# First mixer: modulations 2 to 4 as column-group products on TensorE, with their weights loaded from before the first projection

## The chip, the core and the metric

The kernel runs on one core of one Trainium2 chip. The metric is the device time of one execution in microseconds (us): a median of three runs. Engines go by the profile's names: PE (TensorE matmul) and PEld (its weight load), DVE (VectorE), ACT (ScalarE), POOL (GpSimd), SP (SyncE, which here only issues DMAs). "L498" is line 498 of the kernel before.

## What is computed

A block on 256 tokens of width 1024 (a gated linear attention and a Hyena convolution side by side, then 16 experts), followed by a second block of two layers. The change touches one small product of the first block: the modulation of the layer from the condition vector `c`.

```python
mod_x = split(silu(c) @ w_ada + b_ada, 6)        # c: 1 x 1024, w_ada: 1024 x 6144
p = modulate(rmsnorm(x), mod_x[0], mod_x[1]) @ w_in   # same for ctx, with its own mod
x = x + mod_x[2] * merge(gla(p), hyena(p)) @ w_out
hn = modulate(rmsnorm(x), mod_x[3], mod_x[4])
x = x + mod_x[5] * experts(hn)
```

Modulations 0 and 1 are needed before the projections. Modulation 2 is needed after `w_out`, modulations 3 and 4 at the experts' router and gather, modulation 5 after the experts. Each modulation reads 1024 x 1024 values of `w_ada` (4 MB, four loads of 1 MB) and multiplies them by one vector.

## The kernel before

**Stages of the first mixer** (`mixer1`, L636), in order of the trace. Up to about 47 us: filters and modulations 0 and 1 (`mods`, L436, products on PE in four column groups of 32). From 47 us: `h_transposed(0)` and `(1)` (L715) turn the tokens and the context into `hTh`, `hTl` (high and low halves), while `hy_cols(0)` (L800) and `a_cols` (L859) project them (L1111 to L1113). From about 72 us: `hy_cols(1)` beside `to_tok(0)`, `spectrum(vtok, 0)` and `gates` (L1128). Then `to_tok(1)` and `qk_cols` beside `conv_tok` (L1137), `v_cols` beside `spectrum(x1tok, 1)` (L1140), `g_cols` and `hy_cols(2)` (L1149), `conv_ch`, `w_out`.

**A projection block** (`block`, L746) reads a weight block of 512 columns as two loads of 1 MB from a ring of three slots (`slot`, L220). Each load gives two quarters. A quarter is split by `halves` (L281): ACT writes `wh` (two buffers), then POOL or DVE in turn writes `wl` (three buffers, L276). PE multiplies `wh` with `hTh` and `hTl`, and one quarter later `wl` with `hTh`. While a block runs, the next block's two loads are issued at its second half (`nxt`, L738).

**Modulations 2 to 4** (`mods_x`, L471, called at L1106) run on DVE. Each 1 MB load `wmod` (128 x 2 x 1024) is worked off by two instructions over 128 x 1024 (`scalar_tensor_tensor`, L498; the first of a modulation is a `tensor_scalar`, L496), which add `wmod` times a column of `siluc` to `modacc`. At the end of a modulation PE adds up the partitions with a matrix of ones: 8 products into `modt` for modulations 3 and 4 (result `mcf`), or 2 products of 512 columns into `modb` for modulation 2 (result `m2`), after DVE has added the bias (L513). The steps stand at every second yield of L1128's first generator and every fourth of L1137's. Loads alternate between two rooms, `D8` and `B8`.

**What sets the order.** SP's queue runs in the order in which the program is written (`block1` and `block2` are traced inside a manual schedule for SP). Inside the first mixer, from L1106 on, the order of PE, DVE, ACT and POOL is laid down when the program is built, by a planner that ranks instructions by their place in the program and by its own model of times. On the chip each engine then runs its list strictly in order. `run` (L73) steps generators in turn, `mix(a, b, n)` (L86) steps `b` once per `n` yields of `a`.

**PSUM banks** are handed out by `ps` (L208). Without a number it takes the next one of a cycle (`banks`, L204); with `hold=True` the bank is kept out of the cycle until `free`. A fixed number that is held is replaced by the next of the cycle (`while b is None or b in self.held`). A tile that is given a bank waits until the bank's earlier tile has been read for the last time.

Of the kernel before, what the change touches and what calls it, by code (L numbers as in the profile page):

```python
# [13 lines left out]
F32 = mybir.dt.float32  # L14
# [4 lines left out]
AF = mybir.ActivationFunctionType  # L19
# [4 lines left out]
D = 1024  # L24
# [48 lines left out]
def run(*gens, ratio=1):  # L73

    gens = list(gens)
    while gens:
        for i, g in enumerate(list(gens)):
            for _ in range(1 if i == 0 and len(gens) > 1 else ratio):
                try:
                    next(g)  # L80
                except StopIteration:
                    gens.remove(g)
                    break


def mix(a, b, n):  # L86

    i = 0
    for _ in a:
        yield  # L90
        i += 1
        if i % n == 0:
            next(b, None)
# [76 lines left out]
class K:  # L170
# [265 lines left out]
    def mods(self, m, cols, room):  # L436
# [31 lines left out]
        nc.vector.tensor_copy(cols, pt[:, :16].rearrange("p (k i) -> p k i", i=2))  # L468
        yield

    def mods_x(self, mods, tags, ahead=()):  # L471

        nc, p, A = self.nc, self.m1, self.A
        accs, ahead = {}, deque(ahead)

        def load(m, kp):
            src = A["w_ada"][0, kp * 256:(kp + 1) * 256, m * D:(m + 1) * D].rearrange("(k p) c -> p k c", p=128)
            if not tags:  # L480
                w = self.w(src, [128, 2, D])
                if ahead:
                    self.fetch(*ahead.popleft())
                return w
            wt = p.tile([128, 2, D], F32, name="wmod", tag=tags[kp % len(tags)])
            nc.sync.dma_start(wt, src)
            return wt

        def add(m, kp, out, wt):
            if kp == 0:  # L490
                accs[m] = p.tile([128, D], F32, name="modacc", tag=("idft", "modacc")[m % 2])
            acc = accs[m]
            for kk in range(2):
                c = self.siluc[:, 2 * kp + kk:2 * kp + kk + 1]
                if kp == kk == 0:
                    nc.vector.tensor_scalar(acc, wt[:, kk, :], c, None, op0=ALU.mult)  # L496
                else:
                    nc.vector.scalar_tensor_tensor(acc, wt[:, kk, :], c, acc, op0=ALU.mult, op1=ALU.add)  # L498

        def end(m, out):  # L500
            acc = accs[m]
            if out.shape[1] == 8:
                pt = self.ps("modt")
                for k in range(8):
                    self.mm(pt[:, k:k + 1], acc[:, k * 128:(k + 1) * 128], self.ones[:, 0:1])
                nc.vector.tensor_add(out.rearrange("p (n j) -> p n j", n=2), pt[:, :8].rearrange("p (n j) -> p n j", n=2),
                                     self.badaT[:, 2 * m:2 * m + 2])
            else:
                for nb in range(2):
                    r = 2 * m + nb  # L510
                    pt = self.ps("modb")
                    cs = slice(nb * 512, (nb + 1) * 512)
                    nc.vector.scalar_tensor_tensor(acc[0:12, cs], self.bada, self.ident[0:12, r:r + 1], acc[0:12, cs],  # L513
                                                   op0=ALU.mult, op1=ALU.add)
                    self.mm(pt, self.ones, acc[:, cs])
                    nc.scalar.activation(out[:, nb * 512:(nb + 1) * 512], pt, AF.Copy)

        last, due = None, []
        for m, out in mods:
            for kp in range(4):  # L520
                wt = load(m, kp)
                if last:
                    add(*last)
                if kp == 2 and due:
                    end(*due.pop())
                last = m, kp, out, wt
                yield
            due.append((m, out))
        add(*last)
        yield  # L530
        yield
        end(*due.pop())
# [103 lines left out]
    def mixer1(self):  # L636
        nc, A, m1 = self.nc, self.A, self.m1
# [13 lines left out]
        with self.tc.manual_schedule(engines={mybir.EngineType.PE}):  # L651
# [48 lines left out]
            m2 = m1.tile([128, D], F32, name="m2")  # L700
# [14 lines left out]
        def h_transposed(i):  # L715

            for k in range(8):
                pt = self.ps("tp")[:, 0:256]
                for t in range(2):
                    self.tr(pt[:, t * 128:(t + 1) * 128], (xn, ctx)[i][:, t, k * 128:(k + 1) * 128])  # L720
                tm = m1.tile([128, 256], F32, name="htm", tag=("lae", "aT")[k % 2])
                s_, b_ = sc[:, k, i:i + 1], mc[:, 0, k, i:i + 1]
                nc.scalar.activation(hTh[i][:, k], pt, AF.Identity, scale=s_, bias=b_)
                nc.vector.tensor_scalar(tm, pt, s_, b_, op0=ALU.mult, op1=ALU.add)
                (nc.vector, nc.gpsimd)[k % 2].tensor_tensor(hTl[i][:, k], tm, hTh[i][:, k].bitcast(F32), ALU.subtract)
                yield
# [7 lines left out]
        def flush():  # L734
            while late:
                yield from late.pop(0)
# [4 lines left out]
        def load(c0, j):  # L741
            if (c0, j) not in loaded:
                loaded[c0, j] = self.w(self.cut(W, c0, 512, 4 * j, 4), [128, 4, 512])
            return loaded[c0, j]
# [114 lines left out]
        def a_cols():  # L859

            wt = m1.tile([128, 8, 32], F32, name="wain")
            nc.sync.dma_start(wt, self.cut(W, 1536, 32, 0, 8))
            pts = [self.ps("pa") for _ in range(2)]
            whl = self.hip.tile([128, 1024], F32R, name="whl", tag="wh", bufs=2)[:, :512]
            whl = whl.rearrange("p (k i c) -> p k i c", k=8, i=2)
            self.split(whl[:, :, 0], whl[:, :, 1], wt)
            whl = whl.rearrange("p k i c -> p k (i c)")
            for k in range(8):
                for i in range(2):
                    po = pts[i][:, 0:256]  # L870
                    if k:
                        self.mm(po[0:32], whl[:, k, 0:32], hTl[i][:, k], start=False, stop=False)
                    self.mm(po[0:64], whl[:, k], hTh[i][:, k], start=(k == 0), stop=(k == 7))
                    if k == 0:
                        self.mm(po[0:32], whl[:, k, 0:32], hTl[i][:, k], start=False, stop=False)
                if k % 2:
                    yield
            a4 = m1.tile([64, 512], F32, name="a4", tag="modacc")
            for i in range(2):
                self.copy(a4[:, i * 256:(i + 1) * 256], pts[i][0:64, 0:256])  # L880
            yield
            pt = self.ps("pa")
            self.mm(pt[0:32, :], sel32[0:64], a4)
            nonlocal aT
            aT = m1.tile([33, 512], F32, name="aT", tag="aT")
            nc.vector.memset(aT[32:33, :], 1.0)
            nc.vector.tensor_copy(aT[0:32, :], pt[0:32, :])
# [215 lines left out]
        la = m1.tile([128, 4, 512], F32, name="la", tag="E8")  # L1103
        self.mcf = self.cp.tile([128, 2, 8], F32, name="mcf")
        self.m5 = self.cp.tile([128, D], F32, name="m5", tag="gb")
        mods = self.mods_x(((2, m2), (3, self.mcf[:, 0]), (4, self.mcf[:, 1])), ("D8", "B8"))  # L1106
        self.banks(range(4, 8))

        z7, z5 = [self.room(i, [128, 2, 4, 256], name="uTe") for i in (7, 5)]
        hy0 = hy_cols(0, range(4))  # L1110
        next(hy0)  # L1111
        run(h_transposed(0))
        run(chain(hy0, a_cols(), flush()), h_transposed(1))  # L1113
        mats = self.z6[:, 0:1152].rearrange("p (m c) -> p m c", m=9)
        nc.sync.dma_start(mats, A["k_mats"][:, 0:1152].rearrange("p (m c) -> p m c", m=9))
        both = self.cp.tile([128, 2, 128], F32, name="tri")
# [31 lines left out]
        mods = self.mods_x(((5, self.m5),), (), ((4,), (5, 6)))  # L1148
# [60 lines left out]
        pt = self.ps("wrc")  # L1209
# [1337 lines left out]
```

## Time and profile before

| | |
|---|---|
| time, median of 3 runs | 1628.56 us (1624.29 to 1633.93) |
| the profiled execution | 1633.42 us, of which the span of the trace is 1631.6 us |
| mean granted clock of PE | 0.958 of full speed |
| PE, DVE, ACT, POOL busy in the span | 89%, 44%, 23%, 14% |
| first mixer | from the start to about 291 us, when the experts' first products begin |

The page of the profile gives shares for the whole span. The windows view gives busy time of each engine in a stretch (its ends, its length, then busy us and instructions per engine), with the granted clock, the DMA share and GB/s; the timeline gives single instructions with, in brackets, the idle time of the engine before them and what ended it; the view of waits adds these up by releaser. A product of 32-bit floats shows as two MATMUL records (x8 is four products), one of the projections' split halves as one.

### The profile page before, as it was taken

How to read it: one execution, taken by the hardware profiler on the slowest of the kernel's cores; microseconds unless marked ns; L12 is line 12 of the kernel's file. 1: busy time of each engine (PE TensorE's matmuls, PEld its weight loads, DVE VectorE, ACT ScalarE, POOL GpSimd, SP SyncE). 2: the span in 40 equal slices, each digit the busy share in tenths (PEclk: the TensorE clock that was granted, in tenths of full speed). 3: DMA queues.
4: the chain of work that ended last, by engine and by line, in shares of the span. 5: the costliest groups of instructions: out<-in, count | busy, mean ns of one | idle time of the engine just before them, and what ended most of it. 6: DMA issues, size and time to landing. Idle time of an engine off the chain costs nothing. (4 is left out here: it accounts for less than half of the span.)

```text
span 1631.6 us, 19900 instructions
## 1 busy us (share of the span) xinstructions
PE 1457.9 (89%) x7699; PEld 771.3 (47%) x7705; DVE 712.7 (44%) x1562; ACT 372.8 (23%) x710; POOL 225.3 (14%) x139
## 2 busy tenths in 40 slices
PE   7959898988889888889999989998899999999985
PEld 2738686322224122226777744432367777444321
DVE  7897765001010000018945553432579446543324
ACT  3542243100000000005544311110245443111101
POOL 2472432000000000004212200000132222000000
PEclk9979899999997999999999989999999999899998
DMA  9536557899999999983464568999643645679995
GB/s 370 195 126 255 213 205 308 332 426 425 426 424 425 426 427 427 426 368 123 181 235 165 227 246 317 426 426 425 249 151 140 257 166 210 261 301 425 426 426 211
DMA packets 77463, 497.50 MB, mean 305 GB/s; under 512 B 9082, under 2 KB 9719, under 8 KB 23338
## 3 DMA queue, kind: packets, MB, share of 16 engines
q1 hardware_dynamic: 76136, 492.75, 74.7%
q10 hardware_dynamic: 690, 2.10, 0.3%
q0 software_dynamic: 528, 1.23, 0.3%
q8 instruction: 65, 1.06, 0.3%
q14 instruction: 44, 0.36, 0.1%
HBM read 495.00 MB, written 1.05 MB: 304 GB/s over the span
## 5 line engine op out<-in xcount | busy, mean ns | idle before, releaser
L318 PE MATMUL pg<-w,xsT 128*32 128x512 f32 (+1 forms) x1504 | 302.0, 608 | 25.1 <-DMA w<-in_w_gate_dram 14.4
L276 POOL TENSOR_TENSOR wl<-w,wh 128x1024 fp32r<-128x1024 f32 x47 | 118.5, 2523 | 494.7 <-ACT wh L275 380.1
L318 PEld LDWEIGHTS pg<-w,xsT 128*32 128x32 f32 (+1 forms) x1504 | 78.5, 118 | 203.6 <-issue 136.5
L318 PE MATMUL py<-w,hh 128*32 128x512 f32 x512 | 128.1, 599 | 23.0 <-DMA w<-in_w_down_dram 23.0
L318 PE MATMUL pu<-w,xsT 128*32 128x512 f32 x512 | 126.0, 598 | 17.4 <-DMA w<-in_w_up_dram 17.4
L318 PE MATMUL py<-w,hidT 128*32 128x512 f32 (+1 forms) x496 | 125.9, 624 | 16.0 <-DVE hidT L2282 7.9
L275 ACT ACTIVATE wh<-w 128x1024 fp32r<-128x1024 f32 x98 | 103.3, 1060 | 131.2 <-PE pj L318 50.9
L318 PE MATMUL pj<-wh,xTp 128*128 128x512 f32 (+1 forms) x448 | 123.2, 407 | 0.6 <-ACT cn L1726 0.6
L276 DVE TENSOR_TENSOR wl<-w,wh 128x1024 fp32r<-128x1024 f32 x51 | 73.0, 1432 | 59.0 <-ACT wh L275 45.5
L1407 DVE TENSOR_TENSOR hh<-hh,pu 128x512 f32<-128x512 f32 x8 | 5.4, 687 | 213.5 <-PE pu L318 213.5
L318 PEld LDWEIGHTS pj<-wh,xTp 128*128 128x128 f32 x448 | 80.6, 198 | 19.2 <-issue 3.5
L318 PEld LDWEIGHTS py<-w,hh 128*32 128x32 f32 x512 | 29.7, 108 | 117.5 <-DMA w<-in_w_down_dram 63.4
L1406 ACT ACTIVATE hh<-pg 128x512 f32<-128x512 f32 x8 | 4.8, 597 | 338.1 <-PE pg L318 230.0
L318 PEld LDWEIGHTS py<-w,hidT 128*32 128x32 f32 (+1 forms) x496 | 32.3, 124 | 90.2 <-issue 54.6
L318 PEld LDWEIGHTS pu<-w,xsT 128*32 128x32 f32 x512 | 28.3, 109 | 97.0 <-DMA w<-in_w_up_dram 48.3
L2299 DVE SCALAR_TENSOR_TENSOR yhl<-py,gs,yhl 128x512 fp32r<-128x512 f32 x44 | 32.6, 749 | 94.5 <-ACT yhl L2298 94.5
L1431 DVE SCALAR_TENSOR_TENSOR y<-py,gs,m 128x512 f32<-128x512 f32 x8 | 6.0, 751 | 146.4 <-PE py L318 146.0
L2273 ACT ACTIVATE hid<-pg 128x256 f32<-128x256 f32 x22 | 8.5, 385 | 247.0 <-PE pg L318 247.0
L318 PE MATMUL pj<-wl,xTp 128*128 128x512 f32 (+1 forms) x224 | 60.6, 391 | 0.3 <-DVE wl L276 0.3
L2312 DVE TENSOR_TENSOR y<-y,sct 128x512 f32<-128x512 f32 x88 | 56.1, 681 | 10.6 <-PE sct L318 10.1
L318 PE MATMUL ga<-S,xh 128*128 128x384 f32 (+1 forms) x160 | 53.1, 348 | 5.5 <-DVE S L2223 5.5
L2298 ACT ACTIVATE yhl<-py,gs 128x512 fp32r<-128x512 f32 x44 | 29.8, 687 | 116.0 <-PE py L318 112.2
(628 smaller groups left out, 2381.4 us busy)
## 6 DMA issues: line engine op xcount, KB each, us to landing
w<-in_expert_w_gate_up_dram SPq DMA_DIRECT2D x126, 1024.0 KB, 13.1
w<-in_w_up_dram SPq DMA_DIRECT2D x64, 1024.0 KB, 19.5
w<-in_w_down_dram SPq DMA_DIRECT2D x64, 1024.0 KB, 19.6
w<-in_w_gate_dram SPq DMA_DIRECT2D x62, 1024.0 KB, 19.6
w<-in_expert_w_down_dram SPq DMA_DIRECT2D x62, 1024.0 KB, 14.0
w<-in_w_in_dram SPq DMA_DIRECT2D x38, 1024.0 KB, 5.0
wmod<-in_w_ada_dram SPq DMA_DIRECT2D x12, 1024.0 KB, 5.6
wmod<-in_w_ada_dram SPq DMA_DIRECT2D x13, 512.0 KB, 8.5
```

The source lines that it names most:

```text
L275: nc.scalar.activation(hi, src, AF.Copy)
L276: (eng or nc.vector).tensor_tensor(lo, src, hi.bitcast(F32), ALU.subtract)
L318: self.nc.tensor.matmul(out, lhsT, rhs, start=start, stop=stop)
L1406: nc.scalar.activation(hs, pg[nb], AF.Silu)
L1407: nc.vector.tensor_mul(hs, hs, pu[nb])
L1431: nc.vector.scalar_tensor_tensor(y[:, cs], py[nb], Gs[g][1], m5[:, cs], op0=ALU.mult, op1=ALU.mult)
L2273: nc.scalar.activation(hid, pg[:, 0:256], AF.Silu)
L2298: nc.scalar.activation(yh[:, c], py, AF.Copy, scale=gs)
L2299: nc.vector.scalar_tensor_tensor(yl[:, c], py, gs, yh[:, c].bitcast(F32), op0=ALU.mult, op1=ALU.subtract)
L2312: nc.vector.tensor_add(acc[:, t, c], acc[:, t, c], pt)
```

## The change

`mods_pe` takes the place of `mods_x` for modulations 2 to 4. For each load it issues four products (two halves of the columns, two blocks of rows) with a column of `siluc`, repeated 32 times, as the stationary operand, into the four column groups of one held PSUM bank `modps`. After four loads ACT copies the bank to `modrow`, and the selection matrix `sel` brings the groups together: 8 products into `modt` (then a `tensor_add` with the bias `badaT`), or, for modulation 2, two products of 512 columns into `modb` and two more with 12 rows that add the bias.

The first two loads are issued before `h_transposed(0)`. The next load but one is issued after the products of each load. The steps stand at every third yield of L1113's first generator, then at every second of L1128's, which is 7 and 8 steps of 15. The loads go to `D8` and `C8`, then `D8` and `B8`. The two banks of `a_cols` are now held until they are copied.

```diff
+    def mods_pe(self, mods, tags):
+        nc, p, A = self.nc, self.m1, self.A
+        todo = [(m, kp) for m, _ in mods for kp in range(4)]
+        ahead, tags = deque(), deque(tags)
+        def load(i):
+            if i < len(todo):
+                m, kp = todo[i]
+                ahead.append(p.tile([128, 2, D], F32, name="wmod", tag=tags.popleft()))
+                nc.sync.dma_start(ahead[-1], A["w_ada"][0, kp * 256:(kp + 1) * 256, m * D:(m + 1) * D]
+                                  .rearrange("(k p) c -> p k c", p=128))
+        load(0)
+        load(1)
+        yield
+        for i, (m, kp) in enumerate(todo):
+            wt = ahead.popleft()
+            if kp == 0:
+                pt = self.ps("modps", hold=True)
+            for kk in range(2):
+                c = self.siluc[:, 2 * kp + kk:2 * kp + kk + 1].to_broadcast([128, 32])
+                for nb in range(2):
+                    j = 2 * kk + nb
+                    self.mm(pt[32 * j:32 * j + 32, :], c, wt[:, kk, nb * 512:(nb + 1) * 512], start=(kp == 0), stop=(kp == 3))
+            load(i + 2)
+            yield
+            if kp < 3:
+                continue
+            row = p.tile([128, 512], F32, name="modrow", tag="idft")
+            nc.scalar.activation(row, pt, AF.Copy)
+            self.free(pt)
+            out = dict(mods)[m]
+            if out.shape[1] == 8:
+                pt = self.ps("modt")
+                for k in range(8):
+                    self.mm(pt[:, k:k + 1], row[:, (k % 4) * 128:(k % 4 + 1) * 128],
+                            self.sel[:, 2 * (k // 4):2 * (k // 4) + 1])
+                nc.vector.tensor_add(out.rearrange("p (n j) -> p n j", n=2), pt[:, :8].rearrange("p (n j) -> p n j", n=2),
+                                     self.badaT[:, 2 * m:2 * m + 2])
+            else:
+                for nb in range(2):
+                    r = 2 * m + nb
+                    pt = self.ps("modb")
+                    self.mm(pt, self.sel[:, 2 * nb:2 * nb + 1].to_broadcast([128, 128]), row, start=True, stop=False)
+                    self.mm(pt, self.ident[0:12, r:r + 1].to_broadcast([12, 128]), self.bada, start=False, stop=True)
+                    nc.scalar.activation(out[:, nb * 512:(nb + 1) * 512], pt, AF.Copy)
+            yield
...
-            pts = [self.ps("pa") for _ in range(2)]
+            pts = [self.ps("pa", hold=True) for _ in range(2)]
...
+                self.free(pts[i])
...
-        mods = self.mods_x(((2, m2), (3, self.mcf[:, 0]), (4, self.mcf[:, 1])), ("D8", "B8"))
+        mods = self.mods_pe([(2, m2), (3, self.mcf[:, 0]), (4, self.mcf[:, 1])], ("D8", "C8") * 3 + ("D8", "B8") * 3)
         self.banks(range(4, 8))
...
         hy0 = hy_cols(0, range(4))
         next(hy0)
+        next(mods)
         run(h_transposed(0))
-        run(chain(hy0, a_cols(), flush()), h_transposed(1))
+        run(mix(chain(hy0, a_cols(), flush()), mods, 3), h_transposed(1))
```

## Rows read from the trace of the kernel before

**Rows 1.** Windows: PE, PEld, DVE, ACT, POOL busy, clock, DMA share, GB/s.

```profile
47.10:72.36 25.26, 22.67 (x163) 19.57 (x163) 20.83 (x34) 14.86 (x25) 14.12 (x12) 0.93 0.46 175
72.36:97.10 24.74, 21.52 (x122) 15.12 (x120) 24.64 (x25) 13.85 (x24) 12.40 (x6) 1.00 0.50 170
97.10:119.00 21.90, 7.00 (x29) 4.01 (x28) 21.90 (x17) 8.18 (x11) 20.31 (x9) 0.66 0.42 132
119.00:142.00 23.00, 22.98 (x152) 19.32 (x152) 16.54 (x16) 5.26 (x7) 4.81 (x2) 0.89 0.78 287
142.00:175.60 33.60, 33.59 (x153) 26.55 (x152) 30.34 (x30) 10.99 (x16) 16.47 (x8) 1.00 0.64 241
```

**Rows 2.** Waits of PE, 70 to 126 us: total us, times, longest.

```profile
PE tt L322 <- DVE uTe L813: 14.4, 3, 9.3
PE hyp L318 <- DVE wl L276: 2.9, 1, 2.9
```

**Rows 3.** DVE groups by line, 70 to 154 us: busy us, mean ns.

```profile
L498 DVE SCALAR_TENSOR_TENSOR modacc<-wmod,siluc,modacc 128x1024 f32<-128x1024 f32 x21 | 39.0, 1858 | 0.2
L496 DVE TENSOR_SCALAR modacc<-wmod,siluc 128x1024 f32<-128x1024 f32 x3 | 4.1, 1355 | 0.0
L513 DVE SCALAR_TENSOR_TENSOR modacc<-bada,ident,modacc 12x512 f32<-12x512 f32 x2 | 3.0, 1547 | 0.0
```

**Rows 4.** DVE timeline: start us, us, line and operation, two accumulations.

```profile
71.42 1.28 DVE L498 SCALAR_TENSOR_TENSOR modacc<-wmod,siluc,modacc 128x1024 f32<-128x1024 f32 x1
...
99.18 4.48 DVE L498 SCALAR_TENSOR_TENSOR modacc<-wmod,siluc,modacc 128x1024 f32<-128x1024 f32 x1
```

**Rows 5.** POOL timeline, first spectrum, gates and the next wl.

```profile
87.09 2.13 POOL L925 TENSOR_TENSOR ytm<-X,FB 1x512 f32<-1x512 f32 x1 [9.06 <-DVE ytm L915]
...
98.03 3.33 POOL L926 TENSOR_TENSOR X<-X,ytm 128x1024 f32<-128x1024 f32 x1
...
106.96 1.71 POOL L931 TENSOR_TENSOR Y<-X 128x512 f32<-128x512 f32 x1
108.63 5.56 POOL L975 TENSOR_TENSOR la<-la,uTe 128x1024 f32<-128x1024 f32 x2
114.15 3.34 POOL L276 TENSOR_TENSOR wl<-w,wh 128x1024 fp32r<-128x1024 f32 x1
```

**Rows 6.** PE timeline: prices of products, and the places of three chains.

```profile
21.06 1.07 PE L318 MATMUL modps<-wmod,silu 128*32 128x512 f32 x8
...
78.32 1.13 PE L318 MATMUL dft<-vtok,dft 128*128 128x512 f32 x2
...
107.59 3.46 PE L318 MATMUL modb<-modacc,tri 128*128 128x512 f32 x4 [0.51 <-DVE modacc L513]
...
119.52 1.91 PE L318 MATMUL idft<-X,dft 128*128 128x512 f32 x2
...
138.66 1.84 PE L318 MATMUL modt<-tri,modacc 128*128 128x1 f32 x16
...
181.28 3.78 PE L318 MATMUL bT<-mats,la 128*128 128x256 f32 x8 [5.31 <-DVE v L311]
...
221.64 1.95 PE L318 MATMUL modb<-modacc,tri 128*128 128x512 f32 x4 [0.94 <-DVE modacc L513]
```

**Rows 7.** Timeline of SP's DMA queue around the first projection's loads.

```profile
29.88 28.77 SPq L231 DMA_DIRECT2D w<-in_w_in_dram  x3
58.75 0.38 SPq L862 DMA_DIRECT2D wain<-in_w_in_dram  x1
```

**Rows 8.** ACT timeline: high half of the first projection's third quarter.

```profile
57.03 1.05 ACT L275 ACTIVATE wh<-w 128x1024 fp32r<-128x1024 f32 x1
```

**Rows 9.** The page, DMA issues: KB each, median us to landing.

```profile
wmod<-in_w_ada_dram SPq DMA_DIRECT2D x12, 1024.0 KB, 5.6
```

**Rows 10.** The page, 40 slices of 40.8 us: GB/s that the DMAs moved.

```profile
GB/s 370 195 126 255 213 205 308 332 426 425 426 424 425 426 427 427 426 368 123 181 235 165 227 246 317 426 426 425 249 151 140 257 166 210 261 301 425 426 426 211
```

**Rows 11.** Waits of SP's DMA queue, 0 to 300 us, L263: expert loads.

```profile
SPq L263 <- PE wo L318: 11.8, 1, 11.8
```

## The prediction, made before the change was run

> **What bounds the kernel now.** I read the view of windows first, stage by stage, because the busy shares of the whole span say nothing about one stage. In the stretch that the change is about, 72.36 to 142.0 us (69.64 us), PE is busy for 21.52 + 7.00 + 22.98 = 51.5 us and idle for 18.1 us, nearly all of it between 97.1 and 119.0, where DVE is busy for every microsecond, POOL for 20.31 of 21.9, and PE's granted clock has fallen to 0.66 [rows 1]. The reader is to see that PE is full in the stretch before it and the one after it (33.59 of 33.60 us), and that here it is DVE. The view of waits names who releases PE: 14.4 us in three waits of the transposes `tt` for `uTe`, 2.9 us for a `wl`, both written by DVE [rows 2].
>
> What fills DVE there is the work that the change removes: 39.0 + 4.1 + 3.0 = 46.1 us of the 84 us from 70 to 154 [rows 3]. It costs more than its own length because POOL works beside it: the same accumulation over 128 x 1024 takes 1.28 us early on and 4.48 us while POOL works through the spectrum's chain [rows 4, 5]. PE's order is fixed, so a `tt` that waits for DVE holds all the projections behind it.
>
> After this mixer the kernel is bound by its expert loads: in slices 9 to 17 the DMAs move some 426 GB/s without a break [rows 10], and one of the first expert loads waits 11.8 us for the mixer's last product `wo` [rows 11]. The same number of loads can run ahead of that point before and after, so I take what the mixer gains or loses to reach the end one to one.
>
> **The change, part by part.**
>
> *Removed from DVE:* all 46.1 us. That is worth nothing by itself. It is worth the idle of PE that it causes: at most 18.1 us, plus the time lost at the lower clock that follows the idle. The clock was 0.89 in 119 to 142 and 0.66 in the stretch before, so at full clock the 22.98 us would be some 2.5 us shorter and the 7.00 us, without `modb`, some 1.2 us: 3.7 us.
>
> *Removed and moved on PE:* `modb` leaves this stretch, 3.46 us at the lower clock. One `modt`, 1.84 us, comes in from the next stretch; the other, at 138.66, stays in this one [rows 6].
>
> *Added to PE:* four column-group products for each of twelve loads. The kernel already has this operation: eight records, which is one load's four products, took 1.07 us at full clock [rows 6]. Six loads come into 47 to 72 us and six into 72 to 142: 6.4 us in each. Two more products of `modb` add the bias with 12 rows; I price them like the other two (1.95 us for two at full clock [rows 6]), so modulation 2's end costs 3.9 us, now ahead of 72 us. All of this is on the path, since PE is the engine that then sets the end.
>
> The page "TensorE: Matmul & The Clock Gate" of the Trainium skill, section "Measured speedup vs the span model", speaks against the change here: it measures 3.07 times for four packed tiles and 2.38 for three. Against the 0.98 us of a full-width product in rows 6 the row of 1.07 us for four is 3.7 times. By the page's 3.07 a load would be an estimated 1.28 us and the twelve 2.5 us dearer. The row is of this kernel and the same shapes, so the sum stays with it.
>
> *Stretch 47 to 72 us.* It gains 6.4 + 3.9 = 10.3 us of PE work. PE is idle there for 25.26 − 22.67 = 2.6 us, and the clock of 0.93 costs 1.6 us [rows 1]. The first two loads are issued some 20 us before, so their 2.1 us of products can lie in the idle; half of the clock's loss may return. That leaves 10.3 − 2.1 − 0.8 = 7.4 us; the bounds are 10.3 − 2.6 − 1.6 = 6.1 and, with no cover, 10.3.
>
> *SP's queue.* Here the change adds waits. The second half of the first projection's weights is issued at 29.88 today; the row's other loads and the small `wain` follow it, and the last of the three leaves just before 58.75, when its ring slot is free [rows 7]. After the change the third modulation load stands ahead of that second half, and it waits for the products of the first load, on PE, to free `D8`. Everything queued behind it waits as well. The weights are split at 57.03 [rows 8] and a load takes 5.6 us [rows 9]; the load ahead of it adds some 2.5 us (1 MB at 426 GB/s [rows 10]), so both must leave by about 49 us to be there. The first products can run from 47 us on, in PE's gaps: I take no cost of their own, and up to 4 us if the planner puts them behind the first quarter. That end lies inside the bound of 10.3. Later loads wait two deep on PE: about 6.7 us (5.6 + 1.07) for two loads, some 34 us for the last ten. PE has 22.67 + 21.52 + 22.98 = 67 us of other work in the stretches where they lie [rows 1], so they are covered; without that cover each would be up to 3.4 us of idle.
>
> *PSUM.* The bank held for modulation 3 is one of 4 to 7 when `hy_cols(1)` asks for these by number. By my count of the cycle it is bank 5, so the projection's second column block lands in bank 0 of the other group, which the first spectrum's second `dft` needs too. That `dft`, and what follows from it, must wait until the projection's second block has been evacuated, where the first `dft` now starts at 78.32 us [rows 6]: 72.4 + 7.4 (below) + the 21.5 us of PE work that now stand before 97.1 make 101 us, the new products taking the place of what has to wait. From the first `dft` to the end of POOL's last combination (108.67) it is 30.4 us today [rows 5, 6], so `idft` could start at about 132 us; PE has projections to do until then. A part of the chain is already done by then and POOL is no longer slowed by DVE, so I take 2 us of stall, between 0 and 5.
>
> *After 142 us* the second `modt` is gone: −1.84 us, and the stretch is full of PE work, so it counts. The idle of 5.31 us before `bT`, which waits for DVE's copy of `v` [rows 6], I leave as it is.
>
> The sum: 72 to 142 us −18.1 − 3.7 − 3.5 + 1.8 + 6.4 = −17.1; PSUM stall +2.0; 47 to 72 us +7.4; after it −1.8. Together −9.5 us. Against the profiled execution, 1633.4 us, that is 1623.9. That execution lies 4.9 us above the median of the runs, and nothing in the sum depends on that, so the median becomes 1628.56 − 9.5 = 1619.1 us.
>
> **The rivals.**
>
> *Most of it is given back (about 1625 us).* The stall before `idft` is 5 us and nothing of the 10.3 us is covered, because SP holds the second half of the weights back: −17.1 + 5 + 10.3 − 1.8 = −3.6 us, 1625. For it: the fixed order of PE, which turned such a misjudgement into 14.4 us already [rows 2], and the serial queue. Against it: PE has more independent work in reach than before.
>
> *More is gained (about 1613 us).* The second spectrum's chain also loses DVE work beside it (the last eight accumulations lie after 132 us), so the copy of `v` comes earlier and the 5.31 us before `bT` close; `bT`, 3.78 us for eight records behind the idle, may be shorter by up to half at the full clock: I take 1 us. −9.5 − 6.3 = −15.8 us, 1613. Against it: other work stands ahead of the copy in DVE's fixed order.
>
> *Slower (about 1637 us).* POOL's list becomes the bound. The displaced spectrum ends at 132 us; the gates' two sums take 5.56 us and the next `wl` 3.34 us [rows 5]. If the planner keeps that order, with the `wl` behind them, the `qk` projection gets its first low half at 141 us and not at 117.5 as now. Of the 23 us that PE worked after 119 [rows 1] I take 10 to be still open then: 151 us, which is 9 us later than now; with −1.8 and about a microsecond of late spectrum it is +8.2 us, 1637. It decides from the point where that `wl` stands behind the sums in POOL's list. Against it: POOL would stand idle for long before it, and a planner fills that.
>
> **How the numbers follow.** Forecast 0.45, with its own range 1615 to 1624 (terms 6.1 to 10.3 and 0 to 5, and the spread of the three runs); given back 0.25; more gained 0.18; slower 0.12. Half a per cent, about what a measurement of this kernel can tell from no change, is 8.1 us, so faster begins below 1620.4. Two thirds of the forecast and all of "more gained" lie there: 0.30 + 0.18 = 0.48. The rest of the forecast, "given back" and a little of "slower" lie within: 0.42. Slower keeps 0.10. The range goes from 1610, the third case with the scatter of the runs, to 1632, which leaves most of the last case out.
>
> **What would show it.** Right: in the windows of the changed kernel, DVE is no longer full between 72 and 132 us, the wait of `tt` for `uTe` is gone from the waits of PE, the clock stays near 1.00, and the work that now starts at 142 us starts near 132. The twelve loads' products take about 1.07 us each. `modt` and `modb` stand before 132 us. Wrong, by step: `hyp` products of the second half waiting for `w` or PE for `wmod` (SP's queue); `idft` waiting for POOL (banks); first low half of `qk` late (POOL's list); PE full but starting `pv` later than 136 us (the price of the products); or the mixer ending earlier while the expert stage does not.

## The result: slower by 1.0%

The changed kernel takes 1649.2 us (median; 1638.9 to 1651.2) where the kernel before takes 1631.8 us on the same chip (the 1628.56 us given above is the median of the first three of these executions). The ratio is 1.0102, with a 95% interval of 1.0077 to 1.0126: about 16.6 us slower, taking 1630 us for the whole, as all differences below that come from a ratio do. The forecast was 9.5 us faster, with a range that ended at 1632.

Two profiled executions show where it went. Their spans are 1631.6 and 1646.4 us, and up to the first product of the first projection (`hyp`) they agree: it starts at 50.00 before and at 49.82 after. From there I follow five landmarks in PE's timeline, each as the start of the first such record less the start of the first `hyp`:

| us after the first `hyp` | before | after | later by | added since the last landmark |
|---|---|---|---|---|
| first `dft` of the first spectrum (`vtok`) | 28.3 | 42.9 | 14.6 | +14.6 |
| its first `idft` | 69.5 | 81.4 | 11.9 | −2.7 |
| first `dft` of the second spectrum (`x1tok`) | 92.0 | 110.5 | 18.5 | +6.6 |
| first `bT` | 131.3 | 145.2 | 13.9 | −4.6 |
| first product of the experts (`pg`) | 240.9 | 254.3 | 13.4 | −0.5 |

From `pg` to the end it is 1340.7 us before and 1342.3 after. So the loss arises in two places, ahead of the first spectrum and behind its `idft`, and the experts pass it on nearly one to one.

### The profile page after: what moved, and what is told of

It is laid out like the page before. It is cut to its first block, busy times and chain, and to the rows that moved or that the text cites. A ratio compares the mean times of both kernels' runs of the same rounds, so it can differ in the third digit from the quotient of the medians.

```text
span 1646.4 us, 20064 instructions
## 1 busy us (share of the span) xinstructions
PE 1478.1 (90%) x7799; PEld 777.8 (47%) x7805; DVE 667.6 (41%) x1536; ACT 374.7 (23%) x713; POOL 217.5 (13%) x139
## 5 line engine op out<-in xcount | busy, mean ns | idle before, releaser
L276 DVE TENSOR_TENSOR wl<-w,wh 128x1024 fp32r<-128x1024 f32 x51 | 70.2, 1376 | 69.5 <-ACT wh L275 54.4
L318 PEld LDWEIGHTS pj<-wh,xTp 128*128 128x128 f32 x448 | 80.4, 197 | 19.9 <-issue 3.6
L318 PEld LDWEIGHTS pu<-w,xsT 128*32 128x32 f32 x512 | 28.3, 109 | 95.9 <-issue 47.9
```

Of the source, the lines that this page charges most:

```text
L276: (eng or nc.vector).tensor_tensor(lo, src, hi.bitcast(F32), ALU.subtract)
L318: self.nc.tensor.matmul(out, lhsT, rhs, start=start, stop=stop)
```

## Profile after

The same stretches by the view of windows (length, then busy us of PE, PEld, DVE, ACT and POOL, granted clock, DMA share, GB/s), first of the kernel before, cut at its landmarks:

```profile
50.00:78.32 28.32, 26.47 (x199) 24.18 (x199) 24.38 (x38) 15.84 (x26) 15.77 (x13) 0.95 0.57 211
78.32:119.52 41.20, 23.05 (x103) 13.86 (x103) 41.10 (x31) 18.57 (x28) 30.32 (x13) 0.81 0.42 139
119.52:142.02 22.50, 22.49 (x152) 18.82 (x151) 16.04 (x16) 5.28 (x7) 4.81 (x2) 0.89 0.78 285
```

and of the changed kernel, with the stretch of [rows 1] in which DVE was full:

```profile
49.82:92.74 42.92, 36.27 (x223) 24.31 (x224) 22.30 (x37) 16.22 (x28) 13.34 (x12) 0.93 0.50 184
92.74:131.22 38.48, 32.21 (x204) 20.33 (x202) 16.66 (x20) 20.02 (x29) 15.93 (x9) 0.99 0.74 292
131.22:160.31 29.09, 26.18 (x143) 20.76 (x143) 5.89 (x9) 5.28 (x7) 15.33 (x8) 0.72 0.10 37
...
97.10:119.00 21.90, 19.75 (x132) 13.81 (x131) 10.34 (x15) 11.04 (x17) 4.51 (x3) 1.00 0.97 385
```

The reader is to see that what the change was for did come about: between 97.1 and 119 DVE is busy for 10.34 us and not for 21.90, PE for 19.75 and not for 7.00, at a clock of 1.00 and not 0.66. But PE has 9.8 us more to do ahead of the first spectrum (36.27 against 26.47) and is idle there for 6.65 us where it was for 1.85; and the low clock has moved to the stretch behind `idft`, 0.72 where it was 0.89.

What PE waits for now, from 70 to 165 us (total us, times, longest):

```profile
PE idft L318 <- POOL X L980: 3.9, 1, 3.9
PE dft L318 <- DVE uTe L863: 2.2, 1, 2.2
PE idft L318 <- POOL Y L981: 1.4, 1, 1.4
PE idft L318 <- POOL X L979: 1.4, 1, 1.4
```

The 14.4 us of `tt` for `uTe` [rows 2] are gone. In their place stand waits of the spectrum's own chain. PE's timeline shows both places (start us, us, operation, count; in brackets the idle time before it and what ended it):

```profile
55.89 1.04 PE L318 MATMUL modps<-wmod,siluc 128*32 128x512 f32 x2 [1.05 <-DVE htm L774]
...
58.22 1.06 PE L318 MATMUL modps<-wmod,siluc 128*32 128x512 f32 x6
...
68.36 0.38 PE L318 MATMUL hyp<-hTh,wh 128*128 128x256 f32 x1 [2.52 <-ACT wh L275]
...
79.19 1.02 PE L318 MATMUL modb<-modrow,sel 128*128 128x512 f32 x2
...
114.29 1.10 PE L318 MATMUL dft<-vtok,dft 128*128 128x512 f32 x2 [2.15 <-DVE uTe L863]
...
131.22 2.08 PE L318 MATMUL idft<-X,dft 128*128 128x512 f32 x2 [3.91 <-POOL X L980]
...
134.75 2.07 PE L318 MATMUL idft<-X,dft 128*128 128x512 f32 x2 [1.45 <-POOL X L979]
...
140.13 3.41 PE L318 MATMUL modt<-sel,modrow 128*128 128x1 f32 x16
...
194.97 3.34 PE L318 MATMUL bT<-mats,la 128*128 128x256 f32 x8 [2.55 <-DVE v L311]
```

The first load's products run only at 55.89 and 58.22, in two pieces. A `hyp` at 68.36 waits 2.52 us for its high half. The displaced `dft` stands at 114.29, waiting for the projection's evacuation, as foretold for bank 0, and the chain behind it reaches `idft` only at 131.22, when PE has been idle for 3.91 us; from there the products run at half the clock (0.50 from 131.2 to 146.6; `idft` takes 2.07 us, against 1.02 at the full one below). And SP's queue, in the same view, shows what held the weights:

```profile
30.25 29.45 SPq L483 DMA_DIRECT2D wmod<-in_w_ada_dram  x3
59.75 1.59 SPq L231 DMA_DIRECT2D w<-in_w_in_dram  x3
```

The third modulation load waits for the first one's products, and the second half of the first projection's weights, issued at 29.88 before [rows 7], leaves at 59.75.

## Experiments

All ratios are to the kernel before, on the same chip; in the diffs, "..." marks lines left out. The same landmarks for all kernels (us after the first `hyp`; two values are two profiled executions of one kernel):

| | before | after | banks | queue | both | none | modulation 2 |
|---|---|---|---|---|---|---|---|
| `dft` of `vtok` | 28.3 | 42.9 | 46.7 | 42.2 | 37.7, 39.9 | 28.0 | 27.9, 27.9 |
| first `idft` | 69.5 | 81.4 | 80.4 | 81.8 | 69.5, 74.6 | 51.3 | 57.8, 59.2 |
| `dft` of `x1tok` | 92.0 | 110.5 | 104.4 | 108.4 | 93.9, 100.3 | 78.8 | 81.5, 83.1 |
| first `bT` | 131.3 | 145.2 | 139.1 | 142.9 | 128.5, 135.0 | 113.4 | 118.1, 117.7 |
| first `pg` | 240.9 | 254.3 | 245.6 | 246.3 | 233.1, 242.9 | 215.2 | 227.9, 223.8 |

The two profiles of the kernel with both edits lie up to 9.8 us apart, and PE's granted clock differs where they part: 0.95 and 0.85 between the `dft` of `vtok` and `idft`, 0.95 and 0.92 between `bT` and `pg`. So a single profile is read here for what waits on what, and a size is taken from the ratios.

### The bank put back (e1_banks)

The projection's second column block takes bank 0 by name, where the changed kernel put it by displacement, and the cycle takes bank 5 in its place, so that the spectrum's `dft` needs no bank that a projection holds.

```diff
-        self.banks(range(4))
-        run(mix(chain(hy_cols(1, range(4, 8)), flush()), mods, 2), ...
+        self.banks((1, 2, 3, 5))
+        run(mix(chain(hy_cols(1, (4, 0, 6, 7)), flush()), mods, 2), ...
```

> The changed kernel with one thing undone: the second projection takes banks 4, 0, 6, 7 and the work beside it cycles through 1, 2, 3 and 5, so that the bank held for modulation 3 displaces nothing that the first spectrum needs. Bank theory (the displaced block holds up the first spectrum and idft, and that is most of the loss): the last dft of vtok starts before 102 us and not at 114.3, the first idft before 122 and not at 131.2, the clock does not fall to 0.50 there, and 8 to 14 of the 16.6 us come back, which leaves 3 to 9 us over the kernel before. Queue theory (the late second half of the first projection's weights is most of it): at most 3 us come back. Price theory (the products themselves cost TensorE 15 us and more, and the idle that they were to replace is not there): at most 3 us come back, and idft waits for something else.

Measured: ratio 1.0033 (1.0004 to 1.0062), 5.4 us over before: 11.2 of the 16.6 us come back (0.0069, to about ±0.004). The timeline of PE:

```profile
106.22 1.88 PE L318 MATMUL dft<-vtok,dft 128*128 128x512 f32 x4
...
131.50 0.36 PE L322 MATMUL tt<-ident,uTe 128*128 128x128 f32 x1 [3.56 <-ACT uTe L859]
135.58 1.02 PE L318 MATMUL idft<-X,dft 128*128 128x512 f32 x2
```

This execution's first `hyp` starts 5.4 us later than that of the changed kernel, so 106.22 answers to 100.8 there: the last `dft`, the second product of this row, runs some 12 us ahead of 114.29 and waits for nothing. The place that I expected for `idft` was missed: it stands at +80.4, no earlier than in the changed kernel, because it is behind the projection's work in PE's order. What it no longer does is wait for POOL, so the clock does not fall: 1.02 us and not 2.08. The gain therefore arises behind `idft`: 6.1 us by `x1tok` and by `bT`. These 6.1 us count in a first stretch that is 3.8 us longer in this execution, at a clock of 0.80 and not 0.93; from the `dft` of `vtok` to that of `x1tok` it takes 57.7 us and not 67.6. In the changed kernel the waits that name this chain add up to 2.15 + 3.91 + two of 1.45 = 9.0 us, and the half clock costs about a microsecond for each of four pairs of `idft` and 1.5 for `modt` (3.41 us, against 1.95 for the one before it), some 5.5 us together; less the 3.56 us of `tt` that are left here, that is about 11 us.

### The queue put back (e2_queue)

The second half of the first projection's weights is issued ahead of the modulations' first loads.

```diff
         next(hy0)
+        load(1568, 1)
         next(mods)
```

> The changed kernel with one thing undone: the second half of the first projection's weights is issued ahead of the modulation loads, as it was before the change. Queue theory: the high half of the third quarter is made near 59 us and not at 67.3, the first dft of vtok comes 4 to 7 us earlier, and 4 us or more come back. Bank theory: the same is gained up to the first dft, but the last dft still waits for the second projection's evacuation, so the first idft moves by less than 5 us and 0 to 5 us of the 16.6 come back. Price theory: 0 to 3 us.

Measured: ratio 1.0055 (1.003 to 1.008), 9.0 us over before: some 7.6 us come back. The 2.52 us of `hyp` for `wh` are gone from the waits of PE. The place was missed: the first `dft` of `vtok` comes 0.7 us earlier and not 4 to 7. PE's idle ahead of it does fall, from 6.65 to 3.03 us, but the stretch ran at a clock of 0.82 and not 0.93, and PE's work there took 39.22 us and not 36.27. The profile shows 2.1 us by `x1tok` and 2.3 by `bT`; the rest of what is gained by `pg` arises behind `bT`, which neither edit touches and where the clock was 0.97 and not 0.91. So the queue costs something between 2 and 8 us, and this run leaves the size open.

### Both edits, twice (e3_both, e7_both_again)

> Both of these undone. Bank and queue theory together: 12 to 20 us come back, so the time lies between 4 us over and 4 us under the kernel before, or lower if the 9.5 us that were forecast are there after all. Price theory: it stays 8 us or more over the kernel before, with TensorE busy some 20 us more than before and its idle only some 5 us less.

> The variant with both flaws undone once more, for a narrower interval and a second profile. Its first profile had the mixer's middle, from the first product of the first projection to the first dft of x1tok, 2 us longer than before the change (93.9 against 92.0 us), and the stretch after it 5 us shorter. If that holds, the two together lie 0 to 5 us under the kernel before; if the stretch after it was luck of the clock, at 0 to 4 us over.

Measured: ratios 1.0021 (0.9983 to 1.0059) and 1.0016 (0.9989 to 1.0043); their mean is 3.0 us over before. The two edits together give back 13.6 us, less than the sum of each alone (11.2 + 7.6 = 18.8), so they overlap. SP's queue is as it was meant (first of the two executions):

```profile
27.33 2.78 SPq L231 DMA_DIRECT2D w<-in_w_in_dram  x2
31.12 32.41 SPq L483 DMA_DIRECT2D wmod<-in_w_ada_dram  x3
```

and PE waits neither for the late `wh` nor for POOL any more. Of the two cases named for the second run its time fell into the second: what the first profile gained behind `x1tok` was the clock. And still the change gains nothing: with both of its faults undone it is within what can be measured of the kernel before. Two faults were real, but they were not what stood between this change and a gain.

### No early loads (e4_late)

All twelve loads and their products stand beside `hy_cols(1)`, one step at each yield, and none ahead of the first projection.

```diff
-        mods = self.mods_pe([(2, m2), (3, self.mcf[:, 0]), (4, self.mcf[:, 1])], ("D8", "C8") * 3 + ("D8", "B8") * 3)
+        mods = self.mods_pe([(2, m2), (3, self.mcf[:, 0]), (4, self.mcf[:, 1])], ("D8", "B8") * 6)
...
         next(hy0)
-        next(mods)
...
-        run(mix(chain(hy0, a_cols(), flush()), mods, 3), h_transposed(1))
+        run(chain(hy0, a_cols(), flush()), h_transposed(1))
...
-        run(mix(chain(hy_cols(1, range(4, 8)), flush()), mods, 2), ...
+        next(mods)
+        run(mix(chain(hy_cols(1, range(4, 8)), flush()), mods, 1), ...
```

> The products alone, without the early loads: all modulation loads and products stand beside the second projection, one step at each of its yields, with rooms D8 and B8 only; the first projection and its queue are as before the change, and no bank is held when the second projection asks for its own. Bank and queue theory: both delays are gone; the first stretch ends as before the change (first dft of vtok near 78 us), and the time is 0 to 12 us under the kernel before. Price theory: it is 5 us or more over it, since twelve loads in two rooms and some 13 us of products stand in TensorE's list beside the second projection.

Measured: ratio 1.0048 (1.0018 to 1.0079), 7.8 us over before. The first spectrum is early again (`dft` at +29.1, `idft` at +61.9), but PE now waits for the loads, which come one at a time into two rooms (view of waits):

```profile
PE modps L318 <- DMA wmod<-in_w_ada_dram: 4.1, 2, 2.2
```

The time lies where the price theory had it (5 us or more over) and not where the bank and queue theory did (0 to 12 under). These waits are 4.1 us of the 7.8; so with queue and banks out of the way in another manner, the loads' landing takes part of their place, and the time comes out no better than with both edits.

### None of it (e5_none)

Modulations 2 to 4 are left out altogether, loads, products and sums; their results are set to zero. It bounds what moving them off DVE, with nothing else changed, could give.

> The changed kernel without modulations 2 to 4: their loads, products and sums are left out, and the two results are set to zero. It measures what all of this costs on any engine, since everything else stays. Jam theory (before the change, VectorE's accumulations cost TensorE the 18 us of idle and the lower clock behind it): 14 to 24 us under the kernel before. Price theory (most of that idle has other causes and would be there without the accumulations): 0 to 8 us under it. What the products cost follows from its distance to the variant with both flaws undone: by the sum of rows some 17 us.

Measured: ratio 0.9895 (0.985 to 0.9939), 17.1 us under before (10 to 24 by the interval). The prediction had taken 27.1 us for the same removal (18.1 of idle, 3.7 of clock, 3.5 of `modb`, and 1.8 of `modt` in the stretch behind). The waits of PE show why it is less:

```profile
PE pqk L318 <- DVE x1tok L311: 7.0, 1, 7.0
PE tt L322 <- ACT uTe L859: 4.2, 1, 4.2
PE bT L318 <- DVE v L311: 2.5, 1, 2.5
```

With DVE free, the first spectrum's chain takes 23.3 us from `dft` to `idft` and not 41.2. But PE then stands for 4.2 us before the transposes `tt`, which wait for the projection's evacuation by ACT, and for 7.0 us before a product of `qk` that has nothing to do with `x1tok` but for its bank: the bank holds a `tt`, DVE is to copy it to `x1tok`, and DVE waits for POOL. POOL's timeline and DVE's:

```profile
113.01 4.63 POOL L1026 TENSOR_TENSOR la<-la,uTe 128x1024 f32<-128x1024 f32 x2
```

```profile
117.68 0.69 DVE L311 COPY x1tok<-tt 128x512 f32<-128x512 f32 x1 [8.05 <-POOL la L1026]
```

`x1tok` lies in the room of a summand of the gates' second sum, which ends at 117.64. Of 20.0 us of idle from the first `hyp` to `x1tok` (92.02 less 72.01 busy) 12.4 us are still there (78.80 less 66.45). By `x1tok` the profile shows 13.2 us of gain, where the prediction had 25.3, and by `bT` 17.9. The 25.7 us by `pg` are not a size of the change: between `bT` and `pg` PE is idle for 7.2 us here and 7.4 before, and the clock was 0.98 and 0.90.

The mean of the kernels with both edits is 20.1 us above this one. That is what the new work costs with its faults undone; the prediction had 15.6 us for it (7.4 + 6.4 + 1.8), within the two intervals. It is work, and not waits: up to `x1tok` PE is busy for 87.9 us in the first profile with both edits and for 66.4 here, and idle for 6.1 us and 12.4.

### Modulation 2 alone (e6_m2, e8_m2_again)

What jammed DVE first was modulation 2, whose accumulations end with `modb` at 107.59 in the kernel before [rows 6]. Here only it goes to PE, beside `hy_cols(1)`, with the bank for `modps` taken from the spectrum's group; modulations 3 and 4 stay on DVE, moved on to the next stage, beside `qk_cols`.

```diff
-        mods = self.mods_pe([(2, m2), (3, self.mcf[:, 0]), (4, self.mcf[:, 1])], ("D8", "C8") * 3 + ("D8", "B8") * 3)
+        mods2 = self.mods_pe([(2, m2)], ("D8", "B8") * 2)
+        mods = self.mods_x(((3, self.mcf[:, 0]), (4, self.mcf[:, 1])), ("D8", "B8"))
...
         next(hy0)
-        next(mods)
...
-        run(mix(chain(hy0, a_cols(), flush()), mods, 3), h_transposed(1))
+        run(chain(hy0, a_cols(), flush()), h_transposed(1))
...
-        run(mix(chain(hy_cols(1, range(4, 8)), flush()), mods, 2), ...
+        next(mods2)
+        run(mix(chain(hy_cols(1, range(4, 8)), flush()), mods2, 3), ...
...
-        run(mix(chain(qk_cols(range(6)), flush()), mods, 4), conv_tok(x1tok))
+        run(mix(chain(qk_cols(range(6)), flush()), mods, 2), conv_tok(x1tok))
```

> One part of the change alone: modulation 2 as products on TensorE beside the second projection, its four loads issued only then; modulations 3 and 4 stay accumulations on VectorE, beside the qk projection and after it. TensorE gets 4 x 1.07 + 3.9 us less the old modb, 5 to 6 us, and VectorE loses 20 of the 46 us, those that stood in the full stretch. If the jam is a matter of that stretch alone, 6 to 12 us under the kernel before; if the other 26 us, which now all lie from 119 us on, only move the jam, 0 to 6 us over it.

> The same kernel as the run with modulation 2 alone on TensorE, timed again in more rounds. If its gain of 0.4% is one of the chain and not of chance, the ratio lies between 0.993 and 0.999 again, and the first idft follows the first hyp by 55 to 62 us (69.5 before the change, 57.8 in the first run of this kernel). If the gain was chance, the ratio lies within 0.998 to 1.002 with an interval over 1.

Measured: ratios 0.9962 (0.9933 to 0.999) and 0.9958 (0.993 to 0.9986), 6 to 7 us under the kernel before, and so faster than the kernel before and the changed one. The windows of the second execution, cut at its landmarks:

```profile
54.88:82.78 27.90, 27.67 (x201) 25.66 (x202) 20.17 (x37) 17.12 (x27) 15.88 (x12) 0.91 0.43 158
82.78:114.10 31.32, 28.88 (x118) 13.65 (x118) 17.59 (x21) 18.15 (x28) 23.89 (x13) 0.84 0.54 202
114.10:138.00 23.90, 23.90 (x171) 20.87 (x169) 17.93 (x15) 5.78 (x8) 7.39 (x3) 0.92 0.71 264
```

From the first `hyp` to `x1tok` PE is idle for 2.7 us of 83.1, where it was for 20.0 of 92.0 before. DVE is busy for 17.6 us of the middle stretch and for 17.9 of 23.9 in the last one: there the accumulations of modulations 3 and 4 run without holding PE up. PE takes only the work that fills its own idle time. By `bT` the gain is 13 to 14 us, against 17.9 for leaving everything out, and the time shows half of it. The profile shows one place where some is given back: DVE, full from 165 to 188 us in the second execution, comes late to the copy of `S`, and PE waits 5.7 us for it (1.7 us before, 1.8 without the modulations).

```profile
PE upd L318 <- DVE S L1059: 5.7, 1, 5.7
```

So the jam has partly moved on. In these executions the first `hyp` also comes 8.3 and 4.9 us later than in the one before, at a clock of 0.65 and 0.77 in the 26 to 29 us ahead of it (0.98 before), which no edit touches. Where the rest goes stays open.

### The gates' sums on DVE (e9_none_sums, e10_m2_sums, e11_both_sums)

Is POOL's list what stands behind DVE? The two sums over 128 x 1024 go to DVE, in the kernel without modulations 2 to 4 (results zero), in that with modulation 2 on PE, and in that with both edits.

```diff
-                nc.gpsimd.tensor_tensor(la[:, 2 * j:2 * j + 2], la[:, 2 * j:2 * j + 2], es[j], ALU.add)
+                nc.vector.tensor_tensor(la[:, 2 * j:2 * j + 2], la[:, 2 * j:2 * j + 2], es[j], ALU.add)
```

> The kernel without modulations 2 to 4 (loads, products and sums left out, results zero), and the gates' two sums over 128 x 1024 done by DVE and not by POOL. Theory: the next limit behind the removed work is POOL's list: x1tok lies in the room of one of the summands, so its copy waits for the second sum (113.01 to 117.64 in the run without modulations, copy at 117.68), and with it the bank of tt and PE for 7.0 us. Then PE's wait of 7.0 us for x1tok falls under 2 us, the first dft of x1tok comes 72 to 76 us after the first hyp (78.8 there), and the ratio lies at 0.984 to 0.988 (0.9895 there). Rival: the spectrum's own chain is the limit and the sums only fill a gap: then PE waits 4 us or more for idft or x1tok by another name, and the landmark stays at 77 to 80 us.

> The kernel with modulation 2 alone on TensorE, and the gates' two sums on DVE and not on POOL. Theory (sums on POOL hold x1tok): x1tok's copy comes some 5 us earlier, but PE was idle for only 2.7 us there, so at most 2 us are gained: dft of x1tok at 80 to 83 us after the first hyp (81.5 and 83.1 there), ratio 0.994 to 0.998. Rival (the sums delay the whole stage): the landmark at 76 to 79 us and a ratio of 0.990 to 0.994.

> The changed kernel with the banks and SP's queue put back, and the gates' two sums on DVE and not on POOL. Theory: with both faults undone PE is nearly full there (6 us idle up to x1tok), so freeing POOL is worth 0 to 3 us: ratio 1.000 to 1.003, dft of x1tok 92 to 100 us after the first hyp. Rival (POOL's list is what keeps this change from gaining): the landmark under 91 us, ratio 0.994 to 0.999.

Measured, in this order: ratios 0.9883 (0.9855 to 0.9912), 0.995 (0.9929 to 0.9972) and 1.0015 (0.999 to 1.004); the `dft` of `x1tok` at 77.5, 83.1 and 102.1 us after the first `hyp`. None differs from its kernel with the sums on POOL by more than the intervals. In the first, the wait for `x1tok` is gone, as the theory had it, but the landmark is where the rival had it, and the waits of PE and DVE's timeline say why:

```profile
PE tt L322 <- DVE uTe L863: 9.9, 1, 9.9
```

```profile
95.20 7.42 DVE L1026 TENSOR_TENSOR la<-la,uTe 128x1024 f32<-128x1024 f32 x2 [3.25 <-ACT uTe L1025]
```

The sums, 7.42 us on DVE, hold up the evacuation of `uTe`, and `tt` waits 9.9 us where it waited 4.2. PE's idle up to the landmark is 11.9 us (77.53 less 65.67 busy), as good as the 12.4 before. That longer wait is made by the place to which the sums were moved, so this run does not show what the stage would gain if POOL's sums were out of the way altogether. What the two runs show is that some 12 us of idle stay ahead of the landmark with no accumulation on DVE, behind ACT and POOL in one order and behind DVE in the other. This is why taking all the accumulations away is worth 17 us and not 27. With modulation 2 on PE the time and the landmark are where the theory had them; with both edits the time is, and the landmark is 2 us later than its range.

## Why the prediction was wrong, step by step

The three parts of the sum beside what the runs give for them, each from ratios (to some 5 to 8 us):

| | predicted | measured |
|---|---|---|
| all that is removed | −27.1 | −17.1 (none) |
| the work that is added, without faults | +15.6 | +20.1 (both less none) |
| faults: banks, queue | +2.0 and 0 | +13.6 (after less both) |
| together | −9.5 | +16.6 |

*The PSUM term was mis-sized, by some 9 us.* The displacement was found, with its bank and its wait. That `idft` was put at about 132 us and came at 131.22 is luck: the displaced `dft` was put at 101 us and stood at 114.29, and what follows from it was taken at 30.4 us and took 16.9. It was priced at 2 us (0 to 5) because "PE has projections to do until then". It had none left ahead of `idft` in its order: it waited 9.0 us in four places, and then paid some 5.5 us of half clock, which the prediction had seen in the kernel before (0.89 behind the idle) and did not charge again to an idle of its own making. Undone, the time falls by 11.2 us. The chain itself was also longer than taken: from the first `dft` to the last combination, 30.4 us by [rows 5, 6], it is now 46.7, because one of its inputs comes at 114.29.

*SP's queue was taken at no cost of its own.* The step "the first products can run from 47 us on, in PE's gaps" failed. They were put at 55.89 and 58.22, the weights left at 59.75, which is ten microseconds behind the 49 us that the prediction itself had named as the latest, and `wh` came 2.52 us late for `hyp`. The end of "up to 4 us" held for that wait; the time says 2 to 8.

*The stretch to the first spectrum was outside its bounds*, +14.6 us for 6.1 to 10.3. Six loads' products came there, as said; but the view of groups (49.8 to 92.7 us; busy, mean ns) has 8.3 us for them and not 6.4:

```profile
L318 PE MATMUL modps<-wmod,siluc 128*32 128x512 f32 x48 | 8.3, 603 | 2.2 <-DMA wmod<-in_w_ada_dram 1.2 <-DVE htm L774 1.1
```

Two loads' products were cut into pieces, which costs more than its share (last section). `modb` took 4.2 us (3.9 predicted). And instead of covering 2.6 us, PE's idle grew by 4.8. The step that failed is "their 2.1 us of products can lie in the idle".

*The gain was taken whole, some 10 us too high.* The 18.1 us of idle were all put down to DVE; without the accumulations 7.6 of the 20.0 us up to `x1tok` went. The last wait in front of PE did end with DVE, but others stood close behind: the evacuation of the projection and the gates' sums on POOL, 11.2 us in the run without the modulations, 9.9 when the sums were moved. What is late next when DVE is not entered the sum nowhere; for this stretch only the rival "slower" asked it, of POOL's list.

*What held.* DVE is no longer full there, the wait of `tt` is gone, the clock in that stretch is 1.00. A load's products take 1.06 us (1.07 predicted). The Trainium skill, "TensorE: Matmul & The Clock Gate", section "Measured speedup vs the span model", gives 3.07 times for four packed tiles, which there are row tiles of 32; its row for column tiles has three, at 2.38. For four column groups it is 3.7 here, 1.06 us against 0.98 for one full-width product [rows 6], so the trace's price held and the page's row did not carry over. `modt` and the stretch behind it give 4.6 us: the 1.84 predicted, and half of the idle before `bT`, 5.31 to 2.55, which is the half of the rival "more is gained" that came true, in every kernel run here. The experts pass the rest on one to one.

*The rival "slower" was right in sign and half right in its place.* It put the stop at POOL's list, where the gates' sums stand ahead of what PE needs. POOL's timeline of the changed kernel:

```profile
131.14 2.33 POOL L977 TENSOR_TENSOR X<-X,ytm 128x1024 f32<-128x1024 f32 x1
133.44 1.25 POOL L979 TENSOR_TENSOR X<-Y 128x512 f32<-128x512 f32 x1
134.66 2.33 POOL L1026 TENSOR_TENSOR la<-la,uTe 128x1024 f32<-128x1024 f32 x1
136.96 1.25 POOL L981 TENSOR_TENSOR Y<-X 128x512 f32<-128x512 f32 x1
```

One sum (134.66) does stand inside the spectrum's chain and the third pair of `idft` waits 1.45 us behind it. But the first `idft` waited for the combination that ends at 131.2, late because of the bank, and the `qk` products waited behind `idft` in PE's own order, not for a `wl`. What the sums hold up when PE is not full is `x1tok`, as the run without the modulations shows.

## What to carry to other kernels

Before moving work off a full engine, ask what a kernel without that work would gain, and run it: here it gains some 17 us, and the work in its new place costs some 20. Move only the part that stands in the jam (one modulation of three), and put it where the engine that takes it is idle. And when an idle time is created on PE, charge the slow products behind it as well.

## What the runs showed of the hardware

*A piece of a column-group product costs what the whole costs.* Four products into four column groups take 1.06 us together; the one product that was cut off and ran alone at 55.89 takes 1.04 us, and the three left of that load, at 58.22, 1.06. A planner that slips another instruction between the four pays for the load twice.

*The same idle of PE is followed by either clock.* In the two executions of the kernel with both edits PE waits 2.0 us for the same instruction, and the products after it run at half the clock in one (the first row) and at the full one in the other:

```profile
28.94 2.08 PE L318 MATMUL dft<-eo,dft 128*128 128x512 f32 x2 [2.00 <-DVE FA L681]
```

```profile
28.79 1.12 PE L318 MATMUL dft<-eo,dft 128*128 128x512 f32 x2 [1.99 <-DVE FA L681]
```

The first `hyp` starts at 54.55 in the first and at 49.89 in the second, 4.66 us apart: from these rows to it PE is busy for 22.14 us at a clock of 0.77 in one and for 17.35 at 0.98 in the other. It is why places were compared from the first `hyp` on, and sizes by ratios. The later stretches vary as well, and not the same way: the second execution has the lower clock in them, and from the first `hyp` to `pg` it takes 9.8 us longer.

*POOL is faster when DVE is quiet.* `X<-X,ytm` over 128 x 1024 takes 2.33 us in the changed kernel (the row at 131.14 above) and took 3.33 beside the accumulations [rows 5]. The Trainium skill, "SBUF — State Buffer", section "Who interferes with whom", says that a DVE instruction with two SBUF inputs contends with a GpSimd instruction that reads SBUF, and that the port pair they share is an exclusive lock; the longer times beside DVE agree with it, though no run here shows the lock itself.
